# Score products of the two attention maps side by side in one two-bank tile, and two context tiles in one round

## The chip, the cores and the metric

One core of a Trainium2 chip runs the kernel. The metric is the device time of one execution in microseconds, taken as the median of several runs. The engines are called as in the profile: PE (TensorE, matmuls), DVE (VectorE), ACT (ScalarE), POOL (GpSimd), and SP, which issues most of the transfers. PE's results land in PSUM, eight banks of 128 partitions by 512 numbers of 32 bits.

## The reference

Two layers of a hybrid block over 256 latent tokens and 256 context tokens of 1024 features. In each layer a normed and modulated input goes through one projection whose columns feed three mixers: a Fourier mixer, a gated delta rule in both directions, and differential attention. Gates merge them, a projection and a residual follow, then a squared-ReLU MLP. The last layer leaves the context tokens out where only they would need it. The part that the change touches:

```python
def diff_attend(q, k, v, lam):
    s = jnp.einsum('bqhmd,bkhmd->bhmqk', q, k, preferred_element_type=jnp.float32) * (DA_QK_DIM ** -0.5)
    p = jax.nn.softmax(s, axis=-1)
    a = p[:, :, 0] - lam * p[:, :, 1]
    return jnp.einsum('bhqk,bkhe->bqhe', a.astype(v.dtype), v)
```

There are four heads, and two maps `m` a head with 64 features each. Latent queries see the 512 keys of context and latent tokens, context queries (in layer 0 alone) the 256 keys of the context.

## The kernel before

**Large products.** Every product with weights is made of three matmuls of a 128x128 block, with high and low parts of weights and inputs (`mm3`, L221), summed over eight blocks (`gemm`, L226) in a bank with the tag `pg`. The weights come by DMA (`raw`), ACT makes the high part (L217) and DVE the low one (L218).

**Order.** The program is a list with priorities, from which Tile's scheduler makes a fixed order for each engine. `Weave` (L128) keeps an account of PE's large products in microseconds. A chain of dependent steps (`weave.chain`, L150) takes places in that order: its function `at(t)` gives what follows the priority that the account had at time `t`. The steps of the chain then stand among the large products, and PE works on those while a step waits for DVE or ACT. The delta rule's chain (`dn_chain`, L611) and attention (`attention`, L940) are both placed in this way. `CORE` (L37) holds attention's distances: 2.4 us from the scores to the transposes, 0.8 to the context product, 0.6 to the next round's scores, and 5.0 behind the product with the keys.

**Banks.** The pool `psp` has four tags (`pg`, `pa`, `pd`, `pc`) with two buffers of one bank each, which are all eight banks. Attention takes `pa` (`abank`, L190), the delta rule `pd` and `pc`. The Fourier mixer and the first input products use `pa` as well, before attention starts, and the output products and the MLP after it.

**Attention, a round.** `attention` goes through the query tiles of 128 tokens: tiles 0 and 1 are latent, tiles 2 and 3 context (`nt` is 4 in layer 0 and 2 in layer 1). A round has, for each map `m`, a bank and one matmul over 64 rows, the rows of `q` and `km` at 64 `m` (L957), with 512 columns for latent tiles and 256 for context ones; the maximum (L959) and its scaling (L960) on DVE; and the exponential with its sum on ACT (L963). Then come two reciprocals (L967, L968), a factor (L969) and the combination p0 - lam p1 (L970) on DVE; four (or two) transposes into another bank (L975) and their copy by ACT (L977); four (or two) matmuls with the values into another bank (L982), and their copy into `od` by ACT (L983). With two buffers, the scores of map 0 take the bank that the copy at L977 has read, and those of map 1 the bank that the copy at L983 has read. Behind the rounds are the norm over each row (L986 to L993), the transposes (L998) and the result `yb` (L999, L1000), which the last of the three branches uses (`branch` with `C_GA`, L1080).

**What runs around it.** In each layer, head 0's attention and the first two heads' delta rule run among the products of the Fourier branch, and heads 1 to 3 and the other delta rule among the remaining input products, the first gates of the next branch, and the products with `C_Z` (L1053). Behind them, in layer 0, DVE takes the rows of the conditioning (L299) beside the sums of the branches (L856).

## Time and profile before

| | us |
|---|---|
| median of three runs | 1637.31 |
| lowest and highest | 1635.82, 1639.15 |
| profiled execution, from its first to its last instruction | 1641.3 |
| PE busy | 1568.3 |
| DVE busy | 1192.8 |
| ACT busy | 742.5 |
| POOL busy | 186.1 |

The profile is of one execution of its own, so its span is a little off the median. Busy times of engines overlap each other; PE's matmuls are pipelined, so that a busy PE is not PE at its peak. A 32-bit matmul is two instructions of PE in the trace. All matmuls have the same source line, that of the helper (L142), and are told apart by the tiles that they write and read; `pa<-km,q` are the scores. Some records of matmuls can be missing from a trace.

### The profile page before, as it was taken

The page shows a single profiled execution, that of the slowest core. Times are in us where ns is not written, and L with a number is a line of the kernel's source. Part 1 is how long each engine was busy: PE and PEld are TensorE (multiplying, and loading weights), DVE is VectorE, ACT ScalarE, POOL GpSimd, SP SyncE. Part 2 cuts the span into 40 slices and gives each one's busy share as a digit, 9 for nine tenths or more (in the row PEclk, how much of TensorE's full clock was granted, in tenths as well). Part 3 has the DMA queues.
Part 4 walks back from the last instruction along what each step waited for, and adds up shares of the span by engine and source line. Part 5 has one row for each costly group of instructions (what it writes and reads, how often), then busy time and mean ns, then how long its engine had stood idle before and what let it go on. Part 6 is the DMA issues. An engine that isn't in the chain of part 4 may idle for free.

```text
span 1641.3 us, 26507 instructions
## 1 busy us (share of the span) xinstructions
PE 1568.3 (96%) x10270; PEld 1337.9 (82%) x10270; DVE 1192.8 (73%) x2309; ACT 742.5 (45%) x1533; POOL 186.1 (11%) x196
## 2 busy tenths in 40 slices
PE   5989999999999899999999999799999999999997
PEld 2568878778778788888888888798987889999997
DVE  7686665777779966976767664886777876787675
ACT  3465543575442233432323233465547554555443
POOL 3420100011002203000000003311021102000001
PEclk9989999999999999999999999999999999999998
DMA  6522112320155646466556552231332025556562
GB/s 228 186 87 65 33 62 87 110 65 27 40 182 176 210 152 205 119 195 189 190 180 194 178 180 79 78 119 59 91 108 86 27 85 176 189 168 193 182 188 93
DMA packets 64463, 215.86 MB, mean 132 GB/s; under 512 B 7281, under 2 KB 12305, under 8 KB 64081
## 3 DMA queue, kind: packets, MB, share of 16 engines
q1 hardware_dynamic: 58178, 202.48, 39.0%
q10 hardware_dynamic: 5184, 7.21, 1.3%
q0 software_dynamic: 976, 4.48, 0.9%
q8 instruction: 80, 1.31, 0.3%
q14 instruction: 45, 0.37, 0.1%
HBM read 209.95 MB, written 4.20 MB: 130 GB/s over the span
## 4 chain that ended last, share of the span: by engine, by line
PE 77%; DVE 13%; ACT 4%; DMA 3%; issue 3%; POOL 0%; DVEq 0%; SPq 0%; ACTq 0%; POOLq 0%
PE pg L142 39%; PE pa L142 13%; PE pd L142 13%; PE pc L142 11%; DVE junk L299 3%; DVE cy L594 2%; DVE wlo L218 2%; ACT whi L217 1%; DVE mt L420 1%; DMA raw<-in_wt 1%; PE pc L146 1%; ACT sw L932 1%; PE pa L146 1%; DMA x<-in_xin 0%; DMA raw<-in_wck 0%
## 5 line engine op out<-in xcount | busy, mean ns | idle before, releaser
L218 DVE TENSOR_TENSOR wlo<-raw,whi 128x1024 fp32r<-128x1024 f32 x262 | 326.1, 1245 | 99.8 <-ACT whi L217 96.7
L217 ACT CAST whi<-raw 128x1024 fp32r<-128x1024 f32 x277 | 289.9, 1048 | 226.5 <-PE pg L142 81.3
L142 PE MATMUL pg<-hh,whi 128*128 128x512 f32 (+1 forms) x912 | 325.8, 357 | 1.0 <-DVE gt L856 1.0
L142 PE MATMUL pg<-hh,wlo 128*128 128x512 f32 (+1 forms) x912 | 324.9, 356 | 1.7 <-POOL wlo L218 1.5
L142 PE MATMUL pg<-hl,whi 128*128 128x512 f32 (+1 forms) x912 | 325.0, 356 | 0.0
L299 DVE CUSTOM_DVE_ANT_0 junk<-raw,cb 128x1024 f16<-128x1024 f32 x128 | 161.7, 1263 | 58.5 <-DMA raw<-in_wt 55.1
L142 PEld LDWEIGHTS pg<-hh,whi 128*128 128x128 f32 x912 | 173.0, 190 | 24.7 <-issue 4.2
L142 PEld LDWEIGHTS pg<-hh,wlo 128*128 128x128 f32 x912 | 173.0, 190 | 22.5 <-POOL wlo L218 1.8
L142 PEld LDWEIGHTS pg<-hl,whi 128*128 128x128 f32 x912 | 173.2, 190 | 21.3 <-issue 1.8
L397 POOL TENSOR_TENSOR acc<-acc,sq 128x256 f32<-128x256 f32 x36 | 39.8, 1117 | 597.9 <-ACT sq L395 597.9
L142 PE MATMUL pg<-a,whi 128*128 128x256 f32 (+1 forms) x416 | 102.3, 329 | 0.1
L594 DVE SCALAR_TENSOR_TENSOR cy<-cu,conv,cy 128x512 f32<-128x512 f32 (+1 forms) x96 | 75.7, 789 | 30.5 <-ACT cy L592 29.3
L142 PEld LDWEIGHTS pg<-a,whi 128*128 128x128 f32 x416 | 70.8, 188 | 8.4 <-DVE a L239 0.5
L840 ACT ACTIVATE gt<-pg 128x512 f32<-128x512 f32 (+1 forms) x44 | 21.6, 491 | 110.4 <-PE pg L142 91.1
L142 PE MATMUL pg<-a,wlo 128*128 128x256 f32 (+1 forms) x208 | 68.1, 328 | 0.0
L142 PE MATMUL pc<-a,whi 128*128 128x512 f32 (+1 forms) x224 | 57.4, 337 | 0.1
L142 PE MATMUL pd<-a,whi 128*128 128x256 f32 (+1 forms) x224 | 54.8, 328 | 0.0
L720 ACT CAST Um<-pd 128x512 f16<-128x512 f32 x56 | 34.0, 608 | 42.6 <-PE pd L142 42.1
L142 PE MATMUL pa<-a,whi 128*128 128x256 f32 (+1 forms) x208 | 50.2, 324 | 0.1
L1159 DVE TENSOR_TENSOR mr<-mr 128x512 f32<-128x512 f32 (+1 forms) x64 | 35.4, 555 | 19.0 <-ACT mr L1158 18.8
L142 PE MATMUL pa<-hh,whi 128*128 128x512 f32 (+1 forms) x128 | 49.0, 383 | 0.0
L142 PE MATMUL pa<-hl,whi 128*128 128x512 f32 (+1 forms) x128 | 48.8, 381 | 0.0
(436 smaller groups left out, 3729.2 us busy)
## 6 DMA issues: line engine op xcount, KB each, us to landing
raw<-in_wck SPq DMA_DIRECT2D x280, 512.0 KB, 3.6
raw<-in_wt SPq DMA_DIRECT2D x80, 512.0 KB, 3.7
wv<-in_wt SPq DMA_DIRECT2D x10, 512.0 KB, 3.9
wn<-in_wn SPq DMA_DIRECT2D x16, 192.0 KB, 3.5
x<-in_xin SPq DMA_DIRECT2D x4, 512.0 KB, 9.6
spill<-gt ACTq DMA_DIRECT2D x8, 256.0 KB, 3.8
merged<-spill ACTq DMA_DIRECT2D x8, 256.0 KB, 3.1
cb<-crow POOLq DMA_DIRECT2D x2, 1024.0 KB, 6.3
```

The lines of the kernel that those rows point to most:

```text
L142: self.pe.matmul(out, a, b, start=start, stop=stop)
L146: self.pe.transpose(out, a, ident)
L217: S.copy(hi, r)
L218: eng.tensor_tensor(out=lo, in0=r, in1=hi.bitcast(F32), op=ALU.subtract)
L299: V.tensor_tensor_reduce(out=junk, in0=r, in1=self.cb[:, v], scale=0.5, scalar=0.0, op0=ALU.mult, op1=ALU.add, accum_out=ada[l][:, n, v:v ...
L397: G.tensor_tensor(out=self.acc[s], in0=self.acc[s], in1=q, op=ALU.add)
L420: V.scalar_tensor_tensor(out=t, in0=x[s][:, k], scalar=gain, in1=r[s], op0=ALU.mult, op1=ALU.mult)
L594: V.scalar_tensor_tensor(out=y3, in0=u[:, 0:ns, j:j + L], scalar=conv[:, f, j:j + 1], in1=y3, op0=ALU.mult, op1=ALU.add)
L720: S.copy(uc_, pU.rearrange("p (d b c) -> p d b c", d=2, c=w_))
L840: S.activation(th, ps[:, :n], AF.Tanh, scale=0.5)
L932: S.copy(sw[b:b + 32], ps[b ^ 32:(b ^ 32) + 32, 0:L])
L1159: V.tensor_tensor(out=t, in0=t, in1=t, op=ALU.mult)
```

## The change

- The two score products of a query tile go into one tile of two adjacent banks, map 0 into the first, map 1 into the second. `Weave.matmul` gets an argument `behind`: such a product has the highest priority and an order dependency (without a semaphore) on the product named, so that it stands directly behind it on PE.
- The two context tiles of layer 0 share a round: four products of 256 columns behind each other, in the same two banks, then one round of the rest.
- The maximum of both maps (and both context tiles) is one instruction, so are its scaling and the reciprocal; the factor takes one instruction instead of two of the old ones. The exponentials stay one for each map and tile.
- The transposes go into the first bank of a second two-bank tile, the context products into its second bank; one copy each by ACT.
- `pa` becomes a pool of its own, opened with two buffers of one bank; for attention it is closed and opened with one buffer of two banks, and turned back behind the branches. `psp` gets `reuse_waits="tile"`.
- Comments in the file are removed.

```diff
@@ class Weave
-    def matmul(self, out, a, b, start, stop):
-        self.pe.matmul(out, a, b, start=start, stop=stop)
+    def matmul(self, out, a, b, start, stop, behind=None):
+
+        place = self.tc.cur_priority
+        if behind is not None:
+            self.tc.cur_priority = 0
+        ins = self.pe.matmul(out, a, b, start=start, stop=stop)
+        if behind is not None:
+            self.tc.cur_priority = place
+            self.tc.add_manual_dep(ins.ins, behind.ins.name, mybir.DependencyInfo(mybir.DependencyClass.NoSync, mybir.DependencyReason.DATA), reason="behind")
         self.account(b, 4 if b.dtype == F32 else 1)
+        return ins
@@ body
-    psp = es.enter_context(tc.tile_pool(name="psp", bufs=2, space=bass.MemoryType.PSUM))
+    psp = es.enter_context(tc.tile_pool(name="psp", bufs=2, space=bass.MemoryType.PSUM, reuse_waits="tile"))
...
-        return psp.tile([P, 512], F32, tag=tag, name=tag)
+        return (pap[0] if tag == "pa" else psp).tile([P, 512], F32, tag=tag, name=tag)
+
+
+    pap, pax = [None], ExitStack()
+
+    def pa_banks(name, bufs):
+        pax.close()
+        pap[0] = pax.enter_context(tc.tile_pool(name=name, bufs=bufs, space=bass.MemoryType.PSUM))
+
+    pa_banks("pa", 2)
...
+    def abanks():
+        return pap[0].tile([P, 2, 512], F32, tag="pa", name="pa")
@@ attention
-            rz0 = ap_.tile([P, 4], F32, tag="rz0", name="rz0", bufs=2)
-            for t in range(nt):
-                nk = 4 if t < 2 else 2
-                k0 = 0 if t < 2 else L
-                w_ = nk * P
-                pr, zs = [], []
+            rz0 = ap_.tile([P, 2, 4], F32, tag="rz0", name="rz0", bufs=2)
+
+            for ts in ((0,), (1,), (2, 3))[:2 if last else 3]:
+                ng = len(ts)
+                nk, wt = 4 // ng, 512 // ng
+                k0, tsl = 0 if ng == 1 else L, slice(ts[0], ts[0] + ng)
                 at(t0)
+                ps = abanks()
+                ins = None
+                for i, t in enumerate(ts):
+
+                    for m in range(2):
+                        rows_ = slice(64 * m, 64 * m + 64)
+                        ins = PE.matmul(ps[:, m, i * wt:(i + 1) * wt], q[rows_, t * P:(t + 1) * P], km[rows_, k0:k0 + wt], True, True, ins)
+                mx, z = (ap_.tile([P, 4], F32, tag=t_, name=t_, bufs=2)[:, :2 * ng] for t_ in ("mx", "zz"))
+                pe = ap_.tile([P, 2, 512], F32, tag="pe", name="pe", bufs=1 + last)
+                V.tensor_reduce(out=mx, in_=ps.rearrange("p m (i k) -> p (m i) k", i=ng), axis=AX.X, op=ALU.max)
+                V.tensor_scalar(out=mx, in0=mx, scalar1=-0.125, scalar2=None, op0=ALU.mult)
                 for m in range(2):
-                    ps = abank()
-                    PE.matmul(ps[:, :w_], q[64 * m:64 * m + 64, t * P:(t + 1) * P], km[64 * m:64 * m + 64, k0:k0 + w_], start=True, stop=True)
...
+                    for i in range(ng):
+                        j, sl = m * ng + i, slice(i * wt, (i + 1) * wt)
+                        S.activation(pe[:, m, sl], ps[:, m, sl], AF.Exp, scale=0.125, bias=mx[:, j:j + 1], accum_out=z[:, j:j + 1])
+
+                V.reciprocal(rz0[:, :, tsl], z.rearrange("p (m i) -> p m i", m=2))
+                V.scalar_tensor_tensor(out=z[:, 0:ng], in0=rz0[:, 1, tsl], scalar=nlam, in1=z[:, 0:ng], op0=ALU.mult, op1=ALU.mult)
+                for i in range(ng):
+                    sl = slice(i * wt, (i + 1) * wt)
+                    V.scalar_tensor_tensor(out=pe[:, 0, sl], in0=pe[:, 1, sl], scalar=z[:, i:i + 1], in1=pe[:, 0, sl], op0=ALU.mult, op1=ALU.add)
                 t0 += CORE[0]
                 at(t0)
-                pt = abank()
-                for k in range(nk):
-                    PE.transpose(pt[:, k * P:(k + 1) * P], pr[0][:, k * P:(k + 1) * P], ident)
+                pt = abanks()
+                for k in range(4):
+                    PE.transpose(pt[:, 0, k * P:(k + 1) * P], pe[:, 0, k * P:(k + 1) * P], ident)
                 aT = ap_.tile([P, 4, P], F32, tag="aT", name="aT")
-                S.copy(aT[:, 0:nk], pt[:, :w_].rearrange("p (a b) -> p a b", b=P))
+                S.copy(aT, pt[:, 0].rearrange("p (a b) -> p a b", b=P))
                 t0 += CORE[1]
                 at(t0)
-                po = abank()
-                for k in range(nk):
-                    PE.matmul(po[:, 0:P], aT[:, k], vt[:, k0 // P + k], start=k == 0, stop=k == nk - 1)
-                S.copy(od[:, t], po[:, 0:P])
+                for i in range(ng):
+                    for k in range(nk):
+                        PE.matmul(pt[:, 1, i * P:(i + 1) * P], aT[:, i * nk + k], vt[:, k0 // P + k], start=k == 0, stop=k == nk - 1)
+                S.copy(od[:, tsl], pt[:, 1, 0:ng * P].rearrange("p (a b) -> p a b", b=P))
                 t0 += CORE[2]
@@ mixer
         fnet()
+        pa_banks(f"pa{l}", 1)
...
         ax.close()
+        pa_banks(f"pb{l}", 2)
```

## Rows read from the trace of the kernel before

**Rows 1.** Page: busy time by engine; the chain that ended last, by engine.

```profile
PE 1568.3 (96%) x10270; PEld 1337.9 (82%) x10270; DVE 1192.8 (73%) x2309; ACT 742.5 (45%) x1533; POOL 186.1 (11%) x196
...
PE 77%; DVE 13%; ACT 4%; DMA 3%; issue 3%; POOL 0%; DVEq 0%; SPq 0%; ACTq 0%; POOLq 0%
```

**Rows 2.** Windows: length, busy PE, PEld, DVE, ACT, POOL, clock, DMA share, GB/s.

```profile
190.00:262.00 72.00, 71.11 (x560) 58.47 (x560) 50.48 (x128) 37.41 (x100) 6.54 (x8) 1.00 0.17 56
...
300.00:390.00 90.00, 87.50 (x624) 71.48 (x623) 65.35 (x144) 58.13 (x153) 8.45 (x18) 1.00 0.20 65
...
390.00:490.00 100.00, 98.77 (x636) 74.29 (x635) 77.46 (x203) 50.76 (x136) 4.59 (x5) 1.00 0.30 92
...
520.00:560.00 40.00, 35.61 (x153) 28.27 (x152) 39.30 (x51) 8.94 (x11) 13.28 (x6) 1.00 0.62 208
...
1240.00:1360.00 120.00, 116.82 (x1035) 99.26 (x1034) 96.67 (x247) 73.41 (x183) 12.03 (x12) 1.00 0.22 68
```

**Rows 3.** Tile pa on PE: the score instructions, ns min/median/max, first and last start.

```profile
L142 PE MATMUL pa<-km,q x96: 376/589/693, 211.6 to 1342.4; 64*128 64x512 f32 x64, 64*128 64x256 f32 x32
```

**Rows 4.** Timeline of PE: start, us, operation; score products that stand alone.

```profile
211.64 1.12 PE L142 MATMUL pa<-km,q 64*128 64x512 f32 x2
...
244.98 0.70 PE L142 MATMUL pa<-km,q 64*128 64x256 f32 x2
```

**Rows 5.** Timeline of PE around a pair that stands together, 347 us.

```profile
347.42 0.40 PE L142 MATMUL pg<-hl,whi 128*128 128x512 f32 x1
347.75 1.13 PE L142 MATMUL pa<-km,q 64*128 64x512 f32 x4
348.81 0.50 PE L142 MATMUL pg<-hh,whi 128*128 128x512 f32 x1
349.15 0.39 PE L142 MATMUL pg<-hh,wlo 128*128 128x512 f32 x1
349.38 0.39 PE L142 MATMUL pg<-hl,whi 128*128 128x512 f32 x1
```

**Rows 6.** Timeline of PE, in flight at 347.76 us, and a pair at 378.

```profile
347.75 0.70 PE L142 MATMUL pa<-km,q 64*128 64x512 f32 x2
...
377.93 0.70 PE L142 MATMUL pa<-km,q 64*128 64x256 f32 x4
```

**Rows 7.** Timeline of PE: pairs that stand together, but cost more.

```profile
370.50 1.13 PE L142 MATMUL pa<-km,q 64*128 64x256 f32 x4
...
1302.08 1.55 PE L142 MATMUL pa<-km,q 64*128 64x512 f32 x4
```

**Rows 8.** Timeline of all engines: head 0's first round, and the second's start.

```profile
212.80 0.69 DVE L959 TENSOR_REDUCE mx<-pa 128x1 f32<-128x512 f32 x1 [1.15 <-PE pa L142]
...
214.18 0.69 ACT L963 ACTIVATE pe<-pa,mx 128x512 f32<-128x512 f32 x1 [0.40 <-DVE mx L960]
...
218.14 0.75 DVE L970 SCALAR_TENSOR_TENSOR pe<-pe,zz,pe 128x512 f32<-128x512 f32 x1
...
219.64 0.59 ACT L977 COPY aT<-pa 128x512 f32<-128x512 f32 x1
...
223.37 1.20 PE L142 MATMUL pa<-vt,aT 128*128 128x128 f32 x8
...
224.53 1.12 PE L142 MATMUL pa<-km,q 64*128 64x512 f32 x2
...
225.12 0.29 ACT L983 COPY od<-pa 128x128 f32<-128x128 f32 x1
```

**Rows 9.** Page: the costliest groups of DVE and ACT (mean ns behind busy us).

```profile
L218 DVE TENSOR_TENSOR wlo<-raw,whi 128x1024 fp32r<-128x1024 f32 x262 | 326.1, 1245 | 99.8 <-ACT whi L217 96.7
L217 ACT CAST whi<-raw 128x1024 fp32r<-128x1024 f32 x277 | 289.9, 1048 | 226.5 <-PE pg L142 81.3
```

**Rows 10.** Tile pa on PE: what PE, idle before these instructions, waited for.

```profile
  ACT aT L977: 1.4, 3
```

**Rows 11.** Waits of PE from 490 to 660 us: total, times, longest.

```profile
PE pg L142 <- DVE gt L856: 4.4, 3, 2.5
```

More of the change, by code (lines that the diff above doesn't have):

```diff
@@ L986, in attention @@
             square_sums(od, sso, ap_, "sja")
-            rz = rz0[:, :nt]
+            rz = rz0[:, 0, :nt]
             V.tensor_tensor(out=sso, in0=sso, in1=rz, op=ALU.mult)
@@ L995, in attention @@
             at(t0)
-            pt = abank()
+            pt = abanks()[:, 0]
             for t in range(nt):
@@ L1355, in body @@
     wx.close()
+    pax.close()
     es.close()
```

12 lines of the change are left out of this document (removed).

## The prediction

> **What bounds the kernel now.** I read the page first. TensorE is busy 96% of the span, and the chain of work that ended last runs over PE for 77% of it [rows 1]. Next I cut the span into the stretches in which attention runs [rows 2]: head 0 of layer 0, head 1, heads 2 and 3, and heads 1 to 3 of layer 1 (head 0 of layer 1 lies near 1140 to 1165 us). In them PE stands idle for 72.0 - 71.1 = 0.9, 90.0 - 87.5 = 2.5, 1.2 and 3.2 us, 7.8 us of 382, at a granted clock of 1.00, which is 2.4 GHz. VectorE is at 70 to 81% there and ScalarE at 50 to 65%. So attention is not paced by its own chain of steps: PE fills every wait of it with large products, and what counts in these stretches is how long PE is held. The one stretch that reads otherwise lies just behind, 520 to 560 us, where VectorE is busy 39.3 of 40 us and PE 35.6.
>
> Then I looked at the score products themselves. There are 64 PE instructions of 512 columns and 32 of 256 [rows 3]; a product is two of them, so 32 wide products in 16 pairs and 16 narrow ones in 8 pairs (context tiles of layer 0). I went through all of them in the timeline of PE.
> - Alone, a wide product shows 1.12 us and a narrow one 0.70 [rows 4]. The last 0.07 us of what is shown overlaps the next instruction (1.13 shown, but 348.81 - 347.75 = 1.06 to the next start, [rows 5]), so they hold PE for 1.05 and 0.63. 14 of the 16 wide pairs and 4 of the 8 narrow ones are split in this way, with other products between map 0 and map 1.
> - One wide pair stands together, with both maps in flight at once, and holds PE for 1.06 us: the second map is free [rows 5, 6]. One narrow pair does the same, 0.70 us shown for all four instructions [rows 6].
> - Four pairs stand together but cost more: 1.55 us shown for a wide one and 1.13 for the narrow ones (three like the one shown) [rows 7], 0.42 us over a single product in both widths. A fixed 0.42 us whatever the width is a late start of map 1. These are rounds behind a first round, where map 1 writes the bank that the context product of the round before has just left, so it has a wait of its own (for the copy at L983). The wide pair that is free is a head's first round, whose banks had long been empty.
>
> **The change, part by part.** *Adjacent products.* Both maps now write one tile of two banks, so the wait for a free tile is map 0's; map 1 comes right behind it with none, on the other 64 rows and in another bank. That is the free pair of [rows 5]. Wide: now 28 x 1.05 + 1.06 + 1.48 = 31.9 us, then 16 x 1.06 = 17.0; 14.9 saved. Narrow: now 8 x 0.63 + 3 x 1.06 + 0.63 = 8.9 us. Afterwards four products of 256 columns stand in a row, twice on each half of the rows. No row shows four; I take two narrow slots, 4 x 2 x 0.63 = 5.0 us, so 3.8 saved. The bounds are 1.06 a group, the slot of a wide pair with the same columns (4.6 saved), and four products one after another at 2.52 (1.2 lost); the rows of pairs in flight together are the nearest. In the Trainium skill, "TensorE: Matmul & The Clock Gate", Part 3, a weight load runs under a matmul in flight only when their row groups differ. By that rule the second product on the same rows pays for its load again, as in my 1.26 a group; without it the group would be 1.06 and the sum 0.8 us better.
>
> *Fewer switches.* A score product between large products also costs around itself: the large one ahead holds PE for 0.33 us instead of 0.23, the first one behind for 0.34 [rows 5]. The score products now stand in 42 places (28 + 2 wide, 8 + 4 narrow) and will stand in 20. 22 places fewer at 0.10 (one side only) to 0.21 us are 2.2 to 4.6; I take 3.3, since some stand beside products that have paid for their own switch.
>
> *Context tiles in one round.* Layer 0 has 3 rounds a head instead of 4. Transposes and value products stay the same in number, but stand in 8 places fewer: 0 (if they are split again by the order) to 1.7 us; I take 0.8. Held by PE in all: 14.9 + 3.8 + 3.3 + 0.8 = 22.8 us less.
>
> *VectorE and ScalarE.* One maximum over two banks instead of two of 0.69 us [rows 8]; between 0.69 and 2 x 0.69 us, I take 1.25 from the nearest, VectorE's pass over 1024 columns [rows 9]. Scale and reciprocal are one instruction instead of two, and a pair of context rounds goes from 16 vector instructions to 6. Some 0.5 us a wide round and 2 us a pair of narrow ones, beside PE: nothing by itself. The first exponential now waits for the longer maximum, about 0.6 us later in its round; the same filling products hide that.
>
> *The pools.* `pa` is closed and opened again three times. At the first, the new tile waits for the last split of the Fourier branch; the products for head 0's queries and keys lie between, 24 instructions each at 0.23 us [rows 5], 5.5 us a product in layer 0, so it costs nothing; without them it would be one wait for a copy, 0.6 us like that of [rows 8]. The "tile" waits of `psp` concern a pool that is opened once. No DMA and no queue is moved.
>
> **What comes back.** Less PE work means less cover for the steps of the delta rule that run among the same products. PE waits 7.8 us in these stretches under some 420 us of work; I let it grow by half, 3.3 us (0 if the order closes up, 7.8 if it doubles). And behind layer 0's attention VectorE is the limit: PE has waited 4.4 us there for the branch's sums at L856 [rows 11]. What PE gains in the last rounds of head 3, two narrow pairs with some 1.5 us, finds VectorE still busy, though with about 2 us of attention less; I count 1.0 lost. Net: 22.8 - 3.3 - 1.0 = 18.5 us. The profiled span is 1641.3 us, so it would be 1622.8; what lies around the span isn't shown, and the span alone is 4.0 us above the median, a slow execution by 0.24%. I take the difference to the median: 1637.3 - 18.5 = 1618.8.
>
> **Rivals.** *1. The second map keeps a wait.* If Tile gives map 1 its own wait on the second bank, each pair costs what [rows 7] shows: 31.9 - 16 x 1.48 = 8.2, narrow 8.9 - 4 x 1.68 = 2.2, switches 4.1: 14.5, less 3 coming back: 1626. For it: four of six adjacent pairs are of that kind now. Against: those had two tiles; now there is one.
>
> *2. The cover is gone.* If half of the 22.8 us returns as idle PE (VectorE at 81% in layer 1, and 98% behind layer 0's attention [rows 2]), it is 1637.3 - 10.4 = 1627; all of it would be no change. Against: PE is now idle for only 2% of these stretches although VectorE, ScalarE and the chains are the same, so there is more cover than they need; how much more, the rows don't show.
>
> *3. One tile for the whole round; slower.* Scores, transposes and context products now all take the same single tile. The next round's map 0 cannot start before the copy at L983 has read the last context product; until now only map 1 waited for that, and map 0 needed just the copy at L977. The context products end at 223.37 + 1.20 = 224.57 and that copy at 225.41, 0.84 us later [rows 8]; behind a weight cast of 1.05 us on ScalarE [rows 9] it would be 1.9. Since PE's order is fixed, a stop holds everything queued behind. It decides from 22.8 / 20 = 1.1 us a round; at 1.9 us in all 20 it is 1637.3 - 18.5 + 38 = 1657. Against: PE's instructions on `pa` waited for ScalarE's copies 1.4 us in the whole run [rows 10], and a round has room: the long steps of its path (scores, maximum, two exponentials, combination, copy, context, copy), 1.1 + 1.25 + 1.4 + 0.75 + 0.6 + 1.2 + 0.3, are 6.6 us, while the first two rounds start 224.53 - 211.64 = 12.9 us apart [rows 4, 8]. In the Trainium skill, "TensorEngine Tiling (Array Packing)", PSUM Bottleneck, packing speeds up TensorE but not the emptying of PSUM, which may then be the limit. Here that would be this rival; the trace speaks against it as long as other products fill PE.
>
> **How the numbers follow.** Forecast 0.64; rival 1 0.12; rival 2 0.14, of which 0.04 without a gain that can be told; rival 3 0.07; an order of PE's instructions that shuffles the gain away 0.03. Faster is 0.64 + 0.12 + 0.10 = 0.86, the same 0.07, slower 0.07, where 0.2% (3.3 us) is about what a measurement tells from no change. The range goes from 1611 (the upper terms, 4.6 for switches and narrow groups and 1.7 for the round, with nothing coming back) to 1630 (past rivals 1 and 2).
>
> **What would show it.** Right: four score instructions of 512 columns in about 1.13 us in all 16 wide rounds, eight narrow ones in about 1.3; 20 places; PE's busy time down by about 20 us, most of it in the stretches of [rows 2], layer 0 about 11 us earlier when its mixer ends, the rest in layer 1. Rival 1 shows as 1.55 us a pair, rival 2 as idle PE behind the delta rule's or VectorE's steps, rival 3 as PE waiting for L983 ahead of map 0. I am wrong if pairs are in flight together and PE's span does not shrink with them.

## The result: what was measured, and the profile after

| | before | after |
|---|---|---|
| median, us | 1638.23 (4 runs, 1635.82 to 1642.70) | 1620.52 (4 runs, 1616.73 to 1620.83) |
| ratio, 95% interval | | 0.9878, 0.986 to 0.9896 |
| profiled span, us | 1641.3 | 1618.9 |

The change gains 17.7 us by the medians, 1.2% by the ratio (20.0 us). Below, before and after name the two kernels. The line numbers of the new file are higher: the helper's matmul is L146, its transposes L154, the weights' low and high parts L238 and L237, the branch's sum L876, the maximum L984, the exponential L989, the copies of a round L1002 and L1008, the rows of the conditioning L319.

The page of after: busy time by engine, and the chain that ended last (for [rows 1]).

```profile
PE 1541.4 (95%) x10270; PEld 1327.9 (82%) x10270; DVE 1183.2 (73%) x2221; ACT 738.9 (46%) x1525; POOL 187.9 (12%) x196
...
PE 73%; DVE 15%; ACT 5%; issue 3%; DMA 3%; POOL 0%; DVEq 0%; ACTq 0%; SPq 0%; POOLq 0%
```

PE has the same 10270 instructions and is busy 26.9 us less, 22.0 of it in the two stretches of attention below; VectorE has 88 instructions less and loses 9.6 us. The chain has moved a little from PE to VectorE.

The score products in the timeline of PE, head 0's first round and its context round (for [rows 4 to 7]), and the first maximum on VectorE (for [rows 8]):

```profile
207.06 0.28 PE L146 MATMUL pg<-whi,hl 128*128 128x256 f32 x1
207.27 1.13 PE L146 MATMUL pa<-km,q 64*128 64x512 f32 x4
208.33 0.41 PE L146 MATMUL pd<-id,Tm 128*128 128x64 f16 x8
...
228.68 0.48 PE L146 MATMUL pg<-yl,whi 128*128 128x512 f32 x1
229.09 1.13 PE L146 MATMUL pa<-km,q 64*128 64x256 f32 x8
230.16 0.40 PE L146 MATMUL pd<-Um,E 128*128 128x128 f16 x4
...
208.45 1.23 DVE L984 TENSOR_REDUCE mx<-pa 128x2 f32<-128x1024 f32 x1 [1.17 <-PE pa L146]
```

Four instructions of 512 columns hold PE for 208.33 - 207.27 = 1.06 us, eight of 256 for 1.07. All 16 wide and all 4 context groups look like these, in exactly 20 places. Tile `pa` on PE (for [rows 3] and [rows 10]); the second line is what PE, idle ahead of `pa`, waited for:

```profile
L146 PE MATMUL pa<-km,q x96: 376/589/693, 207.3 to 1319.6; 64*128 64x512 f32 x64, 64*128 64x256 f32 x32
...
  ACT aT L1002: 1.6, 3
```

The single instruction is as long as before (376/589/693 ns); it is their overlap that changed. No wait of PE for the copy at L1008 is listed.

To see where the time went I cut both traces at the same instructions: head 0's first score, the first and the last product of the branch that reads the delta rule (`ydh`), and the first product of the MLP. Windows of before, then of after (columns as in [rows 2]): layer 0's attention; from the last `ydh` of layer 0 to the MLP; layer 1's attention; the `ydh` products of layer 1.

```profile
211.64:497.81 286.17, 282.40 (x1843) 223.50 (x1842) 201.11 (x482) 146.23 (x374) 15.26 (x27) 1.00 0.26 82
546.12:714.21 168.09, 162.57 (x820) 137.87 (x818) 133.02 (x221) 59.61 (x94) 21.48 (x17) 0.98 0.54 174
1139.14:1362.82 223.68, 217.08 (x1867) 189.19 (x1866) 176.81 (x420) 128.17 (x306) 26.86 (x33) 1.00 0.27 80
1362.82:1387.24 24.42, 23.54 (x195) 22.99 (x193) 14.86 (x21) 10.33 (x15) 7.42 (x7) 1.00 0.57 177
```

```profile
207.27:478.50 271.23, 267.24 (x1846) 219.32 (x1846) 193.66 (x417) 144.25 (x367) 15.42 (x27) 1.00 0.26 84
526.68:696.59 169.91, 163.19 (x819) 138.35 (x818) 131.68 (x221) 59.49 (x94) 20.55 (x17) 0.98 0.53 171
1121.34:1339.54 218.20, 210.20 (x1869) 187.43 (x1868) 174.20 (x395) 126.63 (x305) 28.58 (x33) 1.00 0.26 81
1339.54:1365.44 25.90, 23.46 (x192) 22.86 (x192) 15.77 (x22) 11.40 (x16) 8.36 (x7) 1.00 0.59 184
```

Subtracted, with the stretches between them taken from the same records:

| stretch | before | after | difference | of it PE busy | of it PE idle |
|---|---|---|---|---|---|
| layer 0, attention | 286.17 | 271.23 | -14.94 | -15.16 | +0.22 |
| layer 0, `ydh` products | 48.31 | 48.18 | -0.13 | | |
| last `ydh` to the MLP | 168.09 | 169.91 | +1.82 | +0.62 | +1.20 |
| MLP to layer 1's first score | 424.93 | 424.75 | -0.18 | | |
| layer 1, attention | 223.67 | 218.20 | -5.47 | -6.88 | +1.41 |
| layer 1, `ydh` products | 24.42 | 25.90 | +1.48 | -0.08 | +1.56 |
| the rest, to PE's last product | 246.55 | 245.87 | -0.68 | | |

The sum from head 0's first score on is -18.1 us, beside the medians' 17.7. The other 4.4 us of the two spans' difference lie ahead of that score, where PE has the same instructions in the same order in both kernels, and are no part of the change: 3.2 of them in a stretch (107.39 to 132.67) where the profiled execution of before was granted 0.86 of the clock, and that of after 1.00 for the same instructions.

The clock has to be looked at wherever two executions are compared. In the stretch from the last `ydh` to the MLP both of these were granted 0.98, so that its 1.82 us are not the clock's; in some of the runs below it was 0.99 or 1.00 there.

From the same records comes what each kind of instruction holds PE for in the two attention stretches (from its start to the next start, without idle time):

| held, us | before | after | |
|---|---|---|---|
| scores | 24.68 + 16.25 | 12.75 + 8.56 | -19.6 |
| large products | 186.64 + 128.54 | 184.22 + 128.87 | -2.1 |
| delta rule (`pd`, `pc`) | 53.60 + 60.98 | 53.19 + 61.86 | +0.5 |
| transposes and value products | 17.48 + 11.31 | 17.08 + 10.90 | -0.8 |

### The profile page after: what moved, and what is told of

Read it like the earlier page. It is cut to its first block, busy times and chain, and to the rows that moved or that the text cites. A ratio compares the mean times of both kernels' runs of the same rounds, so it can differ in the third digit from the quotient of the medians.

```text
span 1618.9 us, 26446 instructions
## 1 busy us (share of the span) xinstructions
PE 1541.4 (95%) x10270; PEld 1327.9 (82%) x10270; DVE 1183.2 (73%) x2221; ACT 738.9 (46%) x1525; POOL 187.9 (12%) x196
## 4 chain that ended last, share of the span: by engine, by line
PE 73%; DVE 15%; ACT 5%; issue 3%; DMA 3%; POOL 0%; DVEq 0%; ACTq 0%; SPq 0%; POOLq 0%
PE pg L146 35%; PE pd L146 13%; PE pa L146 12%; PE pc L146 11%; DVE junk L319 3%; DVE cy L614 2%; DVE wlo L238 2%; DMA raw<-in_wt 2%; ACT whi L237 1%; DVE mt L440 1%; ACT sw L952 1%; PE pc L154 1%; PE pa L154 1%; DMA wv<-in_wt 0%; DMA x<-in_xin 0%
## 5 line engine op out<-in xcount | busy, mean ns | idle before, releaser
L238 DVE TENSOR_TENSOR wlo<-raw,whi 128x1024 fp32r<-128x1024 f32 x262 | 326.4, 1246 | 99.1 <-ACT whi L237 96.5
L237 ACT CAST whi<-raw 128x1024 fp32r<-128x1024 f32 x277 | 290.1, 1049 | 223.2 <-PE pg L146 79.7
L146 PE MATMUL pg<-hh,whi 128*128 128x512 f32 (+1 forms) x912 | 324.7, 356 | 1.8 <-DVE gt L876 1.8
L146 PE MATMUL pg<-hh,wlo 128*128 128x512 f32 (+1 forms) x912 | 323.9, 355 | 2.0 <-POOL wlo L238 1.5
L146 PE MATMUL pg<-hl,whi 128*128 128x512 f32 (+1 forms) x912 | 323.2, 354 | 0.0
L146 PEld LDWEIGHTS pg<-hh,whi 128*128 128x128 f32 x912 | 172.6, 189 | 23.7 <-issue 3.1
L319 DVE CUSTOM_DVE_ANT_0 junk<-raw,cb 128x1024 f16<-128x1024 f32 x128 | 160.4, 1253 | 41.8 <-DMA raw<-in_wt 38.2
L146 PEld LDWEIGHTS pg<-hh,wlo 128*128 128x128 f32 x912 | 172.7, 189 | 22.0 <-POOL wlo L238 1.8
L146 PEld LDWEIGHTS pg<-hl,whi 128*128 128x128 f32 x912 | 173.0, 190 | 20.7 <-issue 0.8
L146 PE MATMUL pg<-a,whi 128*128 128x256 f32 (+1 forms) x416 | 102.0, 328 | 0.1
L146 PEld LDWEIGHTS pg<-a,whi 128*128 128x128 f32 x416 | 70.7, 188 | 8.4 <-DVE a L259 0.5
L146 PE MATMUL pg<-a,wlo 128*128 128x256 f32 (+1 forms) x208 | 68.0, 327 | 0.0
L146 PE MATMUL pc<-a,whi 128*128 128x512 f32 (+1 forms) x224 | 57.2, 336 | 0.1
L146 PE MATMUL pd<-a,whi 128*128 128x256 f32 (+1 forms) x224 | 54.7, 328 | 0.0
L146 PE MATMUL pa<-a,whi 128*128 128x256 f32 (+1 forms) x208 | 50.0, 324 | 0.1
L146 PE MATMUL pa<-hh,whi 128*128 128x512 f32 (+1 forms) x128 | 48.3, 377 | 0.0
L146 PE MATMUL pa<-hl,whi 128*128 128x512 f32 (+1 forms) x128 | 48.1, 376 | 0.0
```

What stands on the lines that cost most here:

```text
L146: ins = self.pe.matmul(out, a, b, start=start, stop=stop)
L237: S.copy(hi, r)
L238: eng.tensor_tensor(out=lo, in0=r, in1=hi.bitcast(F32), op=ALU.subtract)
L319: V.tensor_tensor_reduce(out=junk, in0=r, in1=self.cb[:, v], scale=0.5, scalar=0.0, op0=ALU.mult, op1=ALU.add, accum_out=ada[l][:, n, v:v ...
```

## The experiments

The theory was that the gain is two maps in flight at once on the two halves of the rows, for which they must stand together and the second must have no wait of its own. Its rivals were that it lies in fewer switches, waits and vector steps, or that the shared context round carries more of it. The ratios below are to the kernel before, run beside each.

### Without the request

```diff
-    ... True, True, ins)
+    ... True, True)
```

> The changed kernel with its two-bank tiles, shared context round and merged vector steps, but without the request that the second product stand directly behind the first; the order is left to the scheduler. In its program 6 of the 16 wide pairs stand adjacent and 10 apart, and the context products form 9 groups instead of 4. Theory (the gain is two maps in flight at once, which needs them adjacent): score products hold PE for 6 x 1.06 + 10 x 2.10 = 27.4 us wide (17.0 in the changed kernel) and about 6.1 us narrow (4.3), and 15 more places at 0.10 to 0.21 us add 1.5 to 3.2: some 14 us lost, about 1635 against 1620.5 with the request and 1638 before. Rival (the gain is in the shared tile, the single wait and the fewer vector instructions, which stay): at most 3 us lost for the places, 1620 to 1624.

Measured: 1637.07 us, ratio 0.999 (0.9978 to 1.0002): the gain is gone. Head 0's first round in the timeline of PE, the two maps 1.9 us apart:

```profile
207.12 1.12 PE L146 MATMUL pa<-km,q 64*128 64x512 f32 x2
...
209.06 1.12 PE L146 MATMUL pa<-km,q 64*128 64x512 f32 x2
```

The scores hold PE for 33.8 us in the attention stretches, against 21.3. That is 12.5 us of the 16.5 by which the two medians differ (expected: 12.2 and 14); the large products of layer 0 hold 2.7 more, 1.6 of it in a stretch (478.07 to 481.48 us) where the granted clock was 0.50, the rest for the switches. PE is idle 2.6 us more there, with one stop of 2.9 us at 477.8, behind a row of the conditioning that VectorE had waited 3.63 us for. The two-bank tile, the shared round and the merged vector steps are all in this kernel; without adjacency they show no gain that the interval tells from none.

### The request alone, in the kernel before

```diff
# Weave.matmul with the argument behind, as in the change
...
+    ins = None    # for each tile
-    PE.matmul(ps[:, :w_], q[...], km[...], start=True, stop=True)
+    ins = PE.matmul(ps[:, :w_], q[...], km[...], True, True, ins)
```

> The kernel before with the request alone: a bank for each map as before, so that the second map has a wait of its own, and rounds of one tile. In its program 6 wide pairs (4 of them without a wait on the second map, all first rounds) and 6 narrow ones (all with a wait) stand adjacent, 36 places instead of 42. Theory (adjacent products are in flight together at full gain only if the second has no wait of its own): wide 4 x 1.06 + 2 x 1.48 + 10 x 2.10 = 28.2 us instead of 31.9, narrow 8.9 as before, places 0.6 to 1.3 less: about 4.6 us gained, 1633.5. In the trace the second map starts about 425 ns behind the first wherever it has a wait, and some 7 ns behind where it has none. Rival (adjacency alone decides and the wait costs nothing): the second map starts some 7 ns behind in all twelve, wide 27.4, narrow 6.3, 8 us gained, 1630.

Measured: 1645.38 us, ratio 1.004 (1.0025 to 1.0054): slower than before, and both numbers missed. The timeline: a first round, whose second map has no wait; then three pairs whose second map waits for the copy of the round before (L991 in this kernel), each with that copy on ScalarE.

```profile
345.83 1.13 PE L146 MATMUL pa<-km,q 64*128 64x512 f32 x4
...
242.54 1.12 PE L146 MATMUL pa<-km,q 64*128 64x256 f32 x4
242.65 0.27 ACT L991 COPY od<-pa 128x128 f32<-128x128 f32 x1 [0.80 <-PE pa L146]
...
1266.38 1.74 PE L146 MATMUL pa<-km,q 64*128 64x512 f32 x4
1266.67 0.27 ACT L991 COPY od<-pa 128x128 f32<-128x128 f32 x1
...
374.97 0.28 ACT L991 COPY od<-pa 128x128 f32<-128x128 f32 x1
375.75 0.70 PE L146 MATMUL pa<-km,q 64*128 64x256 f32 x4
```

In the single records the second map starts 425 ns behind the first at 242.54 and 613 ns at 1266.38, which is 0.05 us behind the end of the copy in both (242.92 and 1266.94 us), as in all six late pairs of this run and all four of the kernel before. At 375.75 the copy had ended half a microsecond earlier, and the second map starts 6 ns behind the first. Of the eight pairs with a wait, six start late (396 to 613 ns) and two don't; the four without start at 6 or 7 ns. So my theory was wrong in one point: a wait does no harm by being there, but by being served late, and it is late where the pair stands right behind the context product whose copy it needs. The constant 0.42 us that I read from [rows 7] is that copy, which there always started 107 ns behind the scores and took some 270, not a price of a wait. In the changed kernel this wait is map 0's, and other products of PE lie in it.

The scores hold PE for 4.4 us less in the attention stretches (36.6 against 40.9), near the 3.7 expected. But PE is idle 3.9 us more in them, and the `ydh` products of layer 1 take 31.7 us instead of 24.4: 23 more large products of other kinds stand among them, and the last head's transposes come 0.5 us behind the first of them instead of 6.7 us ahead. Some 1.6 us of that is the clock, 0.50 from 1362.88 to 1366.29. Why the order came out so much worse wasn't followed further.

### Both maps on the same rows

```diff
-    rows_ = slice(64 * m, 64 * m + 64)
+    rows_ = slice(0, 64)
```

> The changed kernel with both maps computed from the first 64 rows, so map 1's own scores are left out; the order of instructions, waits, tiles and everything behind the scores is as in the changed kernel. The two products now need the same half of the array. Theory (the gain is that two products on different halves of the rows run at once): a wide pair holds PE for about 2.13 us instead of 1.07 and a group of four narrow ones for 2.14 instead of 1.07, 16 x 1.06 + 4 x 1.07 = 21.3 us more, about 1641, a few us less if PE's idle time shrinks with it; all of the gain and a little more is gone although places, waits and vector steps stay merged. Rival (the gain is fewer switches, waits and vector steps): within 2 us of the changed kernel, 1619 to 1623.

Measured: 1635.82 us, ratio 0.998 (0.9967 to 0.9992). The same two groups as shown of after, in the timeline of PE:

```profile
207.15 1.98 PE L146 MATMUL pa<-km,q 64*128 64x512 f32 x4
...
230.67 1.99 PE L146 MATMUL pa<-km,q 64*128 64x256 f32 x8
```

They hold PE for 1.91 and 1.92 us, 17.0 us more in all, and 15.3 of it shows in the medians. The order of instructions, the waits and the tiles are those of after, so this part of the gain is concurrency and nothing else. The 3.4 us that remain against before (1.3 to 5.4 by the interval) are what is left for the 22 places fewer, the shared round and the vector steps. My 2.13 us a pair was too much; the records' start times say why:

```
same rows, wide     0   533   962  1391         (next instruction at 1913)
same rows, narrow   0   320   535   751   967  1183  1399  1615   (1923)
after, narrow       0, 6   320, 326   535, 542   751, 758         (1066)
```

Each half of a product takes 429 ns (512 columns) or 215 (256), the first of a group 105 ns more, and from the last half to the next instruction it is some 93 ns more. These 0.2 us are paid once a place, not once a product; they had looked like part of the product because before almost every product stood alone.

### Context tiles in rounds of their own

```diff
-    for ts in ((0,), (1,), (2, 3))[:2 if last else 3]:
+    for ts in ((0,), (1,), (2,), (3,))[:2 if last else 4]:
```

> The changed kernel with a round for each context tile, as before: 24 score groups instead of 20, 8 more places for transposes and value products, and the vector steps of a narrow round twice. Prediction's terms with the measured group: narrow pairs 8 x 0.63 instead of 4 x 1.07 (0.8 us), 4 places at 0.10 to 0.21 (0.4 to 0.8), the round's other places 0 to 1.7: 1.2 to 3.3 us lost, 1621.7 to 1623.8. Rival (the shared round gives more than that, since layer 0's attention ends later behind a fourth round a head and holds what follows): more than 5 us lost, over 1625.5. Second rival (the shared round gives nothing, VectorE's limit behind layer 0's attention eats it): within 1 us of 1620.5.

Measured: 1627.15 us, ratio 0.9927 (0.9911 to 0.9943), 6.6 us above the changed kernel: the first rival's number. In layer 0's attention the scores hold 1.2 us more and the large products 2.4; 1.4 us of the two together lie in a stretch just behind the stop shown here (466.91 to 470.32 us) where the granted clock was 0.50. PE is idle 2.8 us more, with one stop of 3.56 us (timeline, the last context round of layer 0):

```profile
462.77 1.23 DVE L319 CUSTOM_DVE_ANT_0 junk<-raw,cb 128x1024 f16<-128x1024 f32 x1 [3.40 <-DMA raw<-in_wt]
...
465.84 0.48 DVE L996 SCALAR_TENSOR_TENSOR pe<-pe,zz 128x256 f32<-128x256 f32 x1
...
466.47 0.41 PE L154 MATMUL pa<-kc,pe 128*128 128x128 f32 x2 [3.56 <-DVE pe L996]
```

VectorE waited for a row of the conditioning whose transfer had not landed, the combination (L996 in this kernel) stood behind it, and PE behind that. So this is not yet the price of a round. It also raised the question whether late rows also explain what came back behind layer 0 in the changed kernel, where the timeline shows a stop of the same kind:

```profile
561.75 1.22 DVE L319 CUSTOM_DVE_ANT_0 junk<-raw,cb 128x1024 f16<-128x1024 f32 x1
...
567.29 1.23 DVE L319 CUSTOM_DVE_ANT_0 junk<-raw,cb 128x1024 f16<-128x1024 f32 x1 [4.31 <-DMA raw<-in_wt]
...
570.85 0.68 DVE L876 SCALAR_TENSOR_TENSOR gt<-gt,pg 128x512 f32<-128x512 f32 x1
...
571.58 0.59 PE L146 MATMUL pg<-yh,whi 128*128 128x512 f32 x1 [2.27 <-DVE gt L876]
```

### Rows that need no transfer

```diff
+    one = tp.tile([P, 1024], F32, name="one")
+    nc.sync.dma_start(one, A["wt"][0, 16])
...
-    aw = Rows([(0, i, 2) for i in range(16, 40)], cond_rows(tp), tp)
+    aw = Rows([(0, i, 2) for i in range(16, 40)], cond_rows(tp), tp, one=one)    # each row is this tile
```

The same edit in the kernel before, in the changed kernel, and in the one with context rounds apart.

> The kernel before, with the 24 rows of layer 0's conditioning (L299) behind attention all read from one row loaded once, so their 24 transfers of 512 KB are left out and the conditioning is not the reference's; VectorE's instructions stay. In the kernel before VectorE waits 6.5 us there for these rows (440 to 600 us) and PE 4.4 us for sums behind them. Theory (late rows stop VectorE, and PE behind it): VectorE's waits for rows vanish, PE's waits for the branches' sums fall below 2 us, 1635 or less. Rival (VectorE's own work is the limit, as the prediction said): PE's waits stay at 3 to 5 us, 1637 to 1640.

> The changed kernel with the same edit: the 24 rows from one loaded row, their transfers left out. In the changed kernel VectorE waits 4.3 us for one of the last rows (562.9 to 567.3 us) and PE 2.3 us behind it at 571.6, where the kernel before shows none; 1.9 us of layer 0's gain is lost there. Theory (what came back is the wait for a row's transfer): that wait is gone, and from the first of the branches' products to the last row no more than 0.5 us of the difference between the two kernels with this edit is lost. Rival (it is VectorE's own work): 1 to 2 us of the difference is lost there as without the edit.

> The changed kernel with context rounds of their own (as in the run before), with the 24 rows from one loaded row, their transfers left out. There, the last context round of layer 0 showed PE idle for 3.56 us at 466.5 us, behind a combination that stood on VectorE behind a row whose transfer came 3.40 us late. Theory (more than half of the 6.6 us that the separate rounds cost was this late row, the rest places and switches): with resident rows the separate rounds cost 2 to 4 us against the changed kernel with resident rows, and the stop is gone. Rival (the separate round itself holds PE): 5 to 7 us still.

| | median | ratio, interval | last `ydh` to the MLP |
|---|---|---|---|
| before, rows resident | 1637.15 | 0.9987, 0.9972 to 1.0002 | 166.12 |
| after, rows resident | 1615.68 | 0.9863, 0.9843 to 0.9884 | 163.47 |
| context apart, rows resident | 1619.22 | 0.9885, 0.986 to 0.9909 | 166.51 |

PE's waits for the branches' sums, 440 to 620 us, in the first and the second of these kernels:

```profile
PE pg L142 <- DVE gt L859: 4.0, 3, 2.0
...
PE pg L146 <- DVE gt L879: 2.2, 1, 2.2
```

In the kernel before the transfers are worth little: PE waits 4.0 us instead of 4.4 [rows 11], so the rival is right there, and VectorE's own work is the limit, as the prediction said. In the changed kernel the stop at 571.6 us is gone with the transfers; the one wait left (2.2 us) is at 521.1, where after has one of 2.4. The stretch behind the last `ydh` gains 166.12 - 163.47 = 2.65 us against before instead of losing 1.82, but not all of that is the rows: the granted clock was 0.98 there without the edit in both kernels, and differs with it. Windows of this stretch, with resident rows: before, after, context apart.

```profile
539.74:705.87 166.12, 161.28 (x819) 137.10 (x818) 127.92 (x215) 59.38 (x94) 20.59 (x17) 0.99 0.44 141
527.88:691.34 163.47, 159.65 (x820) 135.87 (x818) 126.12 (x213) 59.37 (x94) 20.05 (x17) 1.00 0.45 142
527.08:693.59 166.51, 162.23 (x820) 138.04 (x818) 127.61 (x212) 59.62 (x94) 21.31 (x17) 0.98 0.44 140
```

Idle time of PE leaves the clock out: after has 1.20 us more of it than before in this stretch (6.72 against 5.52), and 1.02 less with resident rows (3.82 against 4.84). The swing of 2.2 us is about the stop's 2.27. In that profiled execution, then, a late row was what came back behind layer 0. The edit takes the traffic of 24 transfers away too, so by itself it doesn't tell a late row from other transfers held up by these. Whether a row is late in most executions, the times don't settle: with resident rows the two kernels are 21.5 us apart by the medians instead of 17.7, but by the ratios 1.24% instead of 1.22%. The run after next says more.

With resident rows the stop at 466.5 us is gone too, and the separate context rounds cost 3.5 us by the medians instead of 6.6; the intervals of the two ratios overlap. The traces say where. Layer 0's attention takes 272.25 us instead of 270.62: PE is held 2.6 us more (0.9 by scores, 1.4 by large products, 0.6 by the delta rule, 0.3 less by transposes and value products) and idle 1.0 less. The 3.0 us behind the last `ydh` (166.51 against 163.47) are the clock's, 0.98 against 1.00. So the shared round saves PE some 2.6 us of work, 1.6 us of time in this pair of traces, near the 2.2 of the prediction's terms with the measured group; what the medians show beyond that, these traces don't put down to the round.

### A longer hold on the two-bank tile

```diff
+    for _ in range(4):
         S.copy(od[:, tsl], pt[:, 1, 0:ng * P].rearrange("p (a b) -> p a b", b=P))
```

> The changed kernel with the copy of the context product into its result (L1008) done four times, 0.9 us more of ScalarE a round and the single two-bank tile freed that much later; nothing is left out. Theory of the prediction (a round has several us of room, so the single tile does not stop PE): PE's waits for this copy stay under 1 us in the whole run, and the time within 3 us of the changed kernel, 1619 to 1624. Rival (the single tile is handed over at the limit): 0.5 to 0.9 us a round in 20 rounds, 10 to 18 us lost, 1631 to 1639, and PE waits for L1008 ahead of the scores.

Measured: 1626.07 us, ratio 0.9924 (0.9895 to 0.9954), between the two numbers. PE's waits in the whole run:

```profile
PE pa L154 <- DVE od L1019: 2.5, 2, 2.0
...
PE pa L146 <- ACT od L1009: 0.2, 1, 0.2
```

PE waited for this copy (L1009 in this kernel) 0.2 us in all, so the single tile has the room that the prediction gave it. The 5.6 us went elsewhere: 60 more copies are 16 us more of ScalarE, the order shifted with them, and in layer 0 PE is idle 2.1 us more, 2.0 of it at 471.8 us ahead of the transposes of head 3's output. That stop isn't the handover, but it isn't shown to be the busier ScalarE either: VectorE had waited 1.86 us for a row of the conditioning (at 464.4 us) ahead of the steps that PE waited for. What the rest is, no run separates.

### The four context products map by map

```diff
-    for i, t in enumerate(ts):
-        for m in range(2):
+    for m in range(2):
+        for i, t in enumerate(ts):
```

> The changed kernel with the four context products in another order: both tiles of map 0 (rows 0 to 63), then both of map 1, instead of the maps in turn; order of everything else and waits as in the changed kernel, nothing left out. In the changed kernel the four hold PE for 1.07 us, and with all four on the same rows for 1.92 us. Theory (only neighbours on different halves of the rows overlap): of the four, the second and the third overlap, first and fourth stand alone, the group takes about 3 x 0.43 + 0.1 to 0.2 = 1.4 to 1.5 us. Rival (PE starts whatever the other half of the rows can take, in any order): 1.07 us as in the changed kernel. Four groups, so at most 2 us in the whole: the time within 3 us of 1620.5.

```profile
232.35 1.14 PE L146 MATMUL pa<-km,q 64*128 64x256 f32 x8
```

1621.82 us, ratio 0.9891 (0.9868 to 0.9915). The group (timeline of PE) holds PE for 1.07 us as in the changed kernel; its records start in pairs 13 ns apart instead of 6. My theory was wrong: the two products on the other rows, third and fourth in the order, do not wait for the second. (The records don't name the rows. That the second of each pair is on the other half follows from the run on the same rows, where the group took 1.92 us.) It is enough that no product on all rows stands in between.

This run also answers the question of the late row, since all else is in the order of after. VectorE's wait for the same row, and PE's waits from 530 to 600 us:

```profile
568.51 1.23 DVE L319 CUSTOM_DVE_ANT_0 junk<-raw,cb 128x1024 f16<-128x1024 f32 x1 [2.78 <-DMA raw<-in_wt]
...
PE pg L146 <- DVE gt L876: 0.6, 1, 0.6
```

The row was 1.5 us less late, as in the kernel before (2.7 us), and PE did not stop at it (the 0.6 us are at 531.4; after has them too). The stretch from the last `ydh` to the MLP took 166.31 us instead of 169.91. From head 0's first score to the end this execution is 1408.9 us long, 20.8 less than before's 1429.7. Its time is no shorter all the same, since the first score comes at 210.53 us instead of 207.27, at a granted clock of 0.97 up to there against 0.99. So the late row is a matter of the single execution: in this order 2.8 us of it cost PE nothing, and 4.3 cost 3.6 with the slower clock that followed. In other orders 3.0 and 3.4 us (without the request, context apart) stopped PE for 0.6 and 0.8 there, and 3.6 (the last run below) did not.

### Three attempts at a faster version

> The changed kernel with the 24 conditioning rows of layer 0 taken 2 with each of the first 8 products of the branches and 1 with each of the last 8 (TAKE), instead of 2 with 11, then 1, 1 and none with the last 3. Nothing is left out. With resident rows the changed kernel took 1615.7. Theory (rows' transfers come too late at two a product): fewer bytes a product, the stop of 2.3 us before the last rows is gone, 1 to 3 us gained, 1617.5 to 1619.5. Rival (the rows then lie at the very end, and what follows the branches waits for the last of them): 0 to 4 us lost, 1620.5 to 1624.5.

> The changed kernel with the 24 conditioning rows taken 2 with each of the first 12 products and none with the last 4. Theory of late transfers: the same bytes a product, so the wait for a row stays where rows are taken, 4 us of VectorE and 2 to 3 of PE near 565 us: 1619.5 to 1622. Rival (VectorE's own work at the end of the rows is what stops PE, and an earlier end helps): 1 to 2 us gained, 1618.5 to 1619.5.

> The changed kernel with attention's distance from the transposes to the context product at 1.4 instead of 0.8 us (CORE), nothing left out. In the changed kernel PE waits 1.6 us in three places for the copy of the transposes (L1002) ahead of the context products. Theory (PE's waits are single places of the order that a distance can move): those waits go, up to 1.5 us gained, 1619 to 1620.5. Rival (another wait takes their place, since the order of all that follows shifts): within 3 us of 1620.5 on the other side, 1620.5 to 1623.5.

| one line changed | median | ratio, interval | layer 0, attention | last `ydh` to the MLP | MLP to layer 1's first score |
|---|---|---|---|---|---|
| none (after) | 1620.52 | 0.9878, 0.986 to 0.9896 | 271.23 | 169.91 | 424.75 |
| products map by map | 1621.82 | 0.9891, 0.9868 to 0.9915 | 271.32 | 166.31 | 425.45 |
| `TAKE = [2] * 8 + [1] * 8` | 1620.37 | 0.9883, 0.9864 to 0.9903 | 271.27 | 164.78 | 428.37 |
| `TAKE = [2] * 12 + [0] * 4` | 1621.10 | 0.9885, 0.9858 to 0.9911 | 271.35 | 166.41 | 424.94 |
| `CORE = (2.4, 1.4, 0.6, 5.0)` | 1623.35 | 0.9897, 0.9878 to 0.9917 | 274.81 | 166.83 | 423.89 |

None can be told from the changed kernel, and none beats it. Spreading the rows leaves PE's order as it is; the stretch in which they are taken is 5.1 us shorter than in after and 1.5 shorter than in the run map by map, and the next one 3.6 longer. The 1.5 us is the clock, not the rows. Windows of this stretch, map by map and then spread:

```profile
530.17:696.48 166.31, 161.85 (x819) 137.26 (x818) 131.29 (x220) 59.69 (x94) 21.52 (x17) 0.99 0.53 173
526.51:691.29 164.78, 159.99 (x820) 135.84 (x818) 131.40 (x220) 59.38 (x94) 20.93 (x17) 1.00 0.54 175
```

Idle PE is 4.46 and 4.79 us in them. Of the 3.6 us in the next stretch 1.6 is idle PE, and the rest is about what a slower clock took there (0.91 from 691.29 to 710.00). With the rows taken earlier VectorE's longest wait for one is 1.1 us instead of 4.3, but the stretch is as long as in the run map by map, where the row didn't stop PE either. The longer distance removed half of PE's wait for the copy of the transposes (1.6 to 0.8 us) and made layer 0's attention 3.6 us longer, 1.6 of it idle PE. In this run, then, what the distance removed came back at other places of the fixed order.

## Why the prediction was right, point by point

- **The time.** 1618.8 was forecast and 1620.5 measured. The forecast's gain was 18.5 us, the measured one 17.7 by the medians and 18.1 by the account above. That the sum came so near is in part luck, since its errors have both signs: narrow groups gave 0.8 us more, the switches 1.7 less. The 3.3 us for idle time is also not the half of 7.8 that the prediction calls it; half is 3.9.
- **Wide pairs.** All 16 hold PE for 1.06 us, as the one free pair of [rows 5] had; 14.9 us was right. That the shared tile leaves the second map without a wait is the step that it hangs on: after has not one pair with a late second map, and so rival 1 fell. Its 1.55 us a pair were not a constant, though, but a copy that ended late.
- **Narrow groups.** 1.07 us instead of the 1.26 taken: the lower bound, 4.6 us saved instead of 3.8. The step that failed is the reading of 0.63 as a product's own time; 0.2 of it is the edge of a place. By the rule of the Trainium skill, "TensorE: Matmul & The Clock Gate", Part 3, weights load under a matmul in flight only where the row groups differ, and I had priced the second product on the same rows with its load. The trace doesn't agree, and doesn't show that price: in the run on the same rows the halves follow each other at 215 ns whether they belong to one product or to two, and each weight load from the third on (187 ns) starts 1 or 2 ns behind a half in flight on the same rows and ends under it.
- **Switches.** 3.3 us was taken; the large products and the delta rule's hold 2.8 us less in layer 0 and 1.2 more in layer 1, 1.6 in all. This term was mis-sized, by half; what layer 1's products lost is spread over many and has no single row.
- **Context round.** The terms for it are 0.8 us for 8 places fewer, some 0.6 for four places of scores, and with the measured group 0.8 for the scores, 2.2 in all; apart with resident rows the rounds hold PE 2.6 us more. The 0.8 by which transposes and value products hold less in the table above is no proof of the first term: half of it is in layer 1, which has no context round, and with the rounds apart they hold 0.3 us less than together. What places cost shows in the large products and the delta rule (1.4 and 0.6 us).
- **PE held less.** 22.8 us forecast, 15.16 + 6.88 = 22.0 measured.
- **What comes back.** 4.3 us forecast, 4.9 measured (0.22 + 1.82 + 1.41 + 1.48), or 4.4 as idle time alone (0.22 + 1.20 + 1.41 + 1.56), but not where I put it; that the sums agree is luck. The delta rule's chains in layer 0 took 0.2, not their share of 3.3. Layer 1 took 1.4 in its attention and 1.5 in the products behind, where PE waits for the low parts of weights on VectorE (waits of PE, 1330 to 1366 us):

```profile
PE pg L146 <- DVE wlo L238: 1.8, 2, 1.3
PE pg L146 <- DVE gt L876: 0.6, 1, 0.6
```

Before, these were 0.2 and 0.7 us in the same stretch. The 1.0 for a VectorE at its limit behind layer 0 was 1.8 (1.2 of it idle PE), and it is a late transfer, not VectorE's work, and not in every execution (none of it in the run map by map). So layer 0 is 14.9 us earlier when its attention ends and 13.2 at the MLP, not about 11, and layer 1 gives 4, not 7.5.
- **VectorE.** The maximum over two banks takes 1.23 us (1.25 taken), and the first exponential of head 0 starts 3.11 us behind the scores instead of 2.54, 0.57 later (0.6 forecast). The merged steps are all in the run without the request, which shows no gain from them.
- **Rival 2** happened in part: 3.2 us of idle PE in both attention stretches and layer 1's products behind them. **Rival 3** didn't. The copy at L1008 holds up a weight load on `pa` five times, 1.4 us in all (tile `od`, who waited for it), and PE itself never:

```profile
  PEld pa L146: 1.4, 5
```

**What stays open.** Layer 1's 1.5 us wasn't tried: PE's 2.4 us of idle time there were the same in eight versions of the changed kernel, those with resident rows among them (0.7 in the run without the request, whose order is another). One of the four runs of after took 1616.73 us, 3.6 less than the next; whether it is the one without the late row can't be told, since only one execution is profiled.

## What to carry to other kernels

Two products on different halves of the rows are free for each other only if nothing on all rows stands between them and the second has no wait that is served late; give both one tile, so that one wait serves both, and fix their order by hand, since a scheduler that fills gaps with large products may split them (here no gain was left that can be told). Price a short product from a group of them, not from one that stands alone, since a lone one carries the edges of its place. Where an engine's order is fixed, expect part of what PE gains to return as idle time (here 4.4 of 22.0 us), and read one more execution before giving that a cause: here one of the places was a transfer that was late in one profile and not in the next. Before comparing a stretch of two profiles, compare the granted clock in it, or the idle time alone: here a clock of 0.98 instead of 1.00 made 3 us that looked like the cost of a round.

## What the runs showed of the hardware

- Score products on the two halves of the rows start 6 or 7 ns apart, 13 with the maps one after the other, and the pair takes the time of one (1.06 us for 512 columns, both maps).
- A group of 64-row products pays some 105 ns once at its first instruction and 93 behind its last, and 429 ns for each half of 512 columns or 215 for each of 256. In the run on the same rows the weight loads of 187 ns lie under the half ahead of them.
- Behind the stop of 2.27 us (in after, at 571.6 us) PE's next products of 512 columns followed each other at 0.43 us instead of 0.23: the granted clock was 0.54, about its lower level of 1.2 GHz, for 3.5 us, then 0.98 again. Not every such stop is followed by that: one of 2.47 us in the kernel before, at 539.7 us, was not, and behind the same product the changed kernel shows both, with PE's order the same (a stop of 2.39 us in after, of 2.60 in the run with spread rows). Windows: two of after; one of before; behind that product, after and spread.

```profile
571.58:575.10 3.52, 3.52 (x9) 2.77 (x10) 1.81 (x3) 0.00 (x0) 0.00 (x0) 0.54 0.89 292
575.10:580.00 4.90, 4.90 (x23) 4.02 (x22) 2.52 (x3) 1.05 (x1) 0.00 (x0) 0.98 0.28 99
```

```profile
539.70:543.30 3.60, 3.05 (x12) 2.16 (x12) 3.56 (x5) 1.05 (x1) 2.22 (x1) 1.00 0.57 212
```

```profile
519.91:523.90 3.99, 3.99 (x11) 3.13 (x12) 3.96 (x6) 1.05 (x1) 2.21 (x2) 0.59 0.72 217
520.10:524.10 4.00, 3.08 (x13) 2.19 (x13) 3.96 (x6) 1.06 (x1) 2.22 (x2) 1.00 0.68 228
```

So the stop at 571.6 us cost 2.3 us and some 1.6 more, eight products at 0.2 each; 3.6 is what the run map by map, without it, took less in this stretch.
